# Four accumulation banks with written-out roles, and the second LayerNorm given out in single pieces

## The chip, the cores and the metric

One core of a Trainium2 chip runs the whole kernel. The metric is the device time of one execution in microseconds (us), as the median of several runs. TensorE (PE) does the matrix products, VectorE (DVE) the elementwise work and the statistics of the norms, ScalarE (ACT) copies, roundings and tanh, GpSimd (POOL) the reciprocal square roots, and SyncE (SP) issues nearly all DMAs. Each engine works through its own queue in the order in which the program was written. Engines wait for one another by semaphores.

## The reference

One layer of a streaming encoder on 2048 prompt rows and 32 sample rows of 1024 features. This case lives in the last third of it, the SwiGLU block and the norm behind it:

```python
m, states = mixer(h, ...)                               # recurrent, retention and attention heads
h = layer_norm(ALPHA * h + m, p['ln1_g'], p['ln1_b'])
f = swiglu(h, p['w_gate'], p['w_up'], p['w_down'])      # 1024 -> 2816 -> 1024
h = layer_norm(ALPHA * h + f, p['ln2_g'], p['ln2_b'])

def swiglu(h, w_gate, w_up, w_down):
    a = jnp.einsum('btd,df->btf', h, w_gate)
    b = jnp.einsum('btd,df->btf', h, w_up)
    return jnp.einsum('btf,fd->btd', jax.nn.silu(a) * b, w_down)
```

Everything is float32. The kernel keeps that precision by splitting each operand in a rounded high part and a low rest, and adding three products (high x high, low x high, high x low).

## The kernel before

The span has two halves. Until about 1092 us `run()` works through the mixer, and through SwiGLU for the first 288 rows (block 0). The rest is done in two *parts* s = 0 and 1 of 896 rows each (`PART`, block number `NBLK + s`, that is 6 and 7). Per part there are 22 feature tiles f of 128 columns (`FT`). I write (s, f) for one of them.

**The seven products.** `gu(s, f)` computes gate and up projection of one feature tile by a seven-product scheme (Strassen-Winograd): seven products, each of 12 matmuls of 128x448, that are added into four PSUM banks called by the roles x, z, y, v. In the order of the program they are p1 into x, p5 into z, p6 into y, p2 onto x, p4 into v, p7 onto y, p3 onto z. `multiply` issues the 12 matmuls; the elementwise work on the sums (`after_p1` ... `after_p3`, L1575 to L1607, and `low`, L1611) is written one product later, by `behind` and `catch_up`. So `after_p3` of one tile stands in the queues behind p1 of the next. `gbank` takes each bank from a pool of four buffers, one after another; which buffer a new tile gets is left to the pool.

**The weights.** `background(3)` after each product lets ACT round up to some weight tiles (L1390), DVE subtract to get the rest (L1395) and form sums of weights (L1403), and SP load raw weights (L1372, tile `ww`), store the sums (L1414, part 0) or load stored ones back (L1420, part 1).

**Down products.** After p6 of the tile at which a group of feature tiles ends (f = 3 for the first group of three), `down(s, g)` multiplies the group with the down weights: 2 halves x 7 row tiles, each 9 matmuls of 128x512 into one of four `mm` banks, and `d_add` (L1641 for the first group, L1643 later) adds the bank to the row tile `tok`. A row tile is 128 rows x 1024, 512 KB.

**The second norm as side work.** `ln2(b)` is a generator that normalises the finished rows of block b in place and stores them: L492 statistics of two halves, L493, L494, a power on POOL, then L500 and L502, two passes over the whole row tile. L505 stores it, and only when the store has landed does `load_rows` (L168) load the next part's rows into the freed tile. `y0` = `ln2(0)` has three tiles and runs in (0, 1) to (0, 3); `y6` = `ln2(6)` has seven and runs in (1, 0) to (1, 3). Of the next part's seven row tiles two are loaded at the start of `y6`, and five wait for a store. The last part's norm is written out in `finale`.

**What sets the order.** The order in each queue is fixed when the program is built. `step()` is called after each product and each row tile of `down`. It adds `pace["rate"]` (us of DVE work) to a credit that is kept up to 1.0, and calls `next` on the side generators while the credit is positive; the number that a generator yields is taken off. `pipeline(gens, 2)` starts the next row tile at every second call, and a call advances *all* active row tiles by one stage each. In `down`, a loop advances the norm until the row tile needed is loaded; in the second half it runs the norm to its end.

Where lines of the changed kernel are shown, they stand higher by 2 to 12: 492 became 494 and 496, 493 became 497, 494 498, 500 504, 502 506, 505 509, 1372 1383, 1395 1406, 1403 1414, 1420 1431, 1567 1578, 1589 1600, 1595 1606, 1602 1613, 1603 1614 and 1641 1653.

Of the kernel before, what the change touches and what calls it, by code (L numbers as in the profile page):

```python
# [9 lines left out]
F32 = mybir.dt.float32  # L10
# [21 lines left out]
NBLK = len(BLOCKS)  # L32
# [65 lines left out]
def tile_hybrid_step(ctx: ExitStack, tc: tile.TileContext, io, outs):  # L98
# [33 lines left out]


    tok, arrived = {}, {}
    side, express, pace = {}, {}, {"rate": 1.5, "credit": 0.0, "turn": [], "twice": False, "factor": 1.0, "turns": 0}

    def row_tile():
        return tk.tile([128, D], F32, name="tok", bufs=11)
# [150 lines left out]
    def step():  # L289

        for name, n in list(express.items()):
            for _ in range(n):
                if name in side:
                    advance(name)
        pace["turns"] += 1
        pace["credit"] = min(pace["credit"], 1.0) + pace["rate"]
        for name in pace["turn"][:]:
            if pace["credit"] <= 0.0:
                break
            pace["turn"].remove(name)  # L300
            pace["turn"].append(name)
            pace["credit"] -= advance(name)
# [4 lines left out]
        while pace["turns"] < until:  # L307
            yield 0.0

    def pipeline(gens, every):  # L310

        gens, active, n = list(gens), [], 0
        while gens or active:
            if gens and n % every == 0:
                active.append(gens.pop(0))
            cost = 0.0
            for g in active[:]:
                try:
                    c = next(g)
                    cost += 0.5 if c is None else c  # L320
                except StopIteration:
                    active.remove(g)
            n += 1
            yield cost
# [149 lines left out]
    def ln2(b):  # L474

        after = max(b, NBLK - 1) + 1
        ahead = 11 - 2 - len(ttiles(b))
        mine = tok[b]
        gt, bt = bcast("ln2_g"), bcast("ln2_b")
        here = pace["turns"] + 5  # L480
        n = len(ttiles(b))
        st = sb.tile([128, n, 2, 6], F32, name="ln_st", bufs=2)
        mv = sb.tile([128, n, 2], F32, name="ln_mv", bufs=2)
        rs = sb.tile([128, n], F32, name="ln_rs", bufs=2)
        more = list(range(len(ttiles(after)))) if after < NBLK + NPART else []
        for _ in range(min(ahead, len(more))):
            load_rows(after, (more.pop(0),))

        def tile_(t, c0, rows):
            x = mine[t][:rows, :]  # L490
            for i in range(2):
                dve.bn_stats(st[:rows, t, i, :], x[:, i * 512:(i + 1) * 512])  # L492
            dve.bn_aggr(mv[:rows, t, :], st[:rows, t])  # L493
            dve.tensor_scalar(rs[:rows, t:t + 1], mv[:rows, t, 1:2], EPS, None, op0=ALU.add)  # L494
            yield 1.75
            pool.tensor_tensor(rs[:rows, t:t + 1], rs[:rows, t:t + 1], mhalf[:rows, 0:1], op=ALU.pow)  # L496
            yield 0.1
            while pace["turns"] < here:
                yield 0.0
            dve.scalar_tensor_tensor(x, x, mv[:rows, t, 0:1], gt[:rows, :], op0=ALU.subtract, op1=ALU.mult)  # L500
            yield 1.35
            dve.scalar_tensor_tensor(x, x, rs[:rows, t:t + 1], bt[:rows, :], op0=ALU.mult, op1=ALU.add)  # L502
            yield 1.35
            if c0 < ptok(b):
                sp.dma_start(outs["y"][START[b] + c0:START[b] + c0 + 128, :], x)  # L505
            else:
                sp.dma_start(outs["ys"], x)
            mine[t] = None
            if more:
                load_rows(after, (more.pop(0),))  # L510
            yield 0.0

        yield from pipeline([tile_(t, c0, rows) for t, (c0, rows) in enumerate(ttiles(b))], 2)
        del gt, bt
        while more:
            load_rows(after, (more.pop(0),))
        del tok[b]
# [725 lines left out]
        loads()  # L1243
        start("w0", (need([(0, 0, n)]) and None for n in ("b11", "t1", "t2")))

    def gbank(n=HALF):
        return pg.tile([128, 512], F32, name="gu", bufs=4)[:, :n]

    def two():
        return xp.tile([128, 2, HALF], F32, name="two", bufs=4)  # L1250
# [294 lines left out]
    def behind(*fns):  # L1545

        lag.append(fns)
# [8 lines left out]
    def gu(s, f):  # L1556

        bank, v = {}, {}

        def multiply(n, left, right, first):  # L1560
            if first:
                bank[n] = gbank()
            (wl, wh), = need([(s, f, right)])
            xl, xh = X[left]
            for x, (w, a) in enumerate(((wh, xh), (wl, xh), (wh, xl))):
                for k in range(4):
                    pe.matmul(bank[n], w[:, k * 128:k * 128 + 128], a[:, k, :],  # L1567
                              start=first and x == 0 and k == 0,
                              stop=x == 2 and k == 3, skip_group_check=not first)
            drop([(s, f, right)])  # L1570

        def after_p1():
            x = two()
            v["t1"], v["g1"] = x[:, 0, :], x[:, 1, :]
            act.activation(v["t1"], bank["x"], AF.Copy)  # L1575

        def after_p5():
            x = v["raw"] = two()
            v["u2"], v["p5"] = x[:, 0, :], x[:, 1, :]
            act.activation(v["p5"], bank["z"], AF.Copy)  # L1580

        def after_p6():
            dve.tensor_tensor(v["u2"], v["t1"], bank["y"], op=ALU.add)

        def after_p2():
            act.activation(v["g1"], bank["x"], AF.Tanh, scale=0.5)

        def after_p4():
            dve.scalar_tensor_tensor(v["g1"], v["g1"], 1.0, bank["x"], op0=ALU.add, op1=ALU.mult)

        def after_p7():
            x = two()
            v["c"], v["g2"] = x[:, 0, :], x[:, 1, :]
            v["u3"] = v["t1"]
            dve.tensor_tensor(v["u3"], v["t1"], bank["y"], op=ALU.add)  # L1595
            dve.tensor_tensor(v["c"], v["u3"], bank["v"], op=ALU.subtract)
            dve.tensor_tensor(v["p5"], v["u3"], v["p5"], op=ALU.add)
            act.activation(v["g2"], v["c"], AF.Tanh, scale=0.5)

        def after_p3():  # L1600
            t = GT[f] = xp.tile([128, 2, PART], F32R, name="g", bufs=3)
            dve.tensor_tensor(v["u2"], v["u2"], bank["z"], op=ALU.add)
            dve.scalar_tensor_tensor(v["u2"], v["g1"], 0.5, v["u2"], op0=ALU.mult, op1=ALU.mult)
            dve.scalar_tensor_tensor(v["g2"], v["g2"], 1.0, v["c"], op0=ALU.add, op1=ALU.mult)
            act.activation(t[:, 1, :HALF], v["u2"], AF.Copy)
            dve.scalar_tensor_tensor(v["p5"], v["g2"], 0.5, v["p5"], op0=ALU.mult, op1=ALU.mult)
            act.activation(t[:, 1, HALF:], v["p5"], AF.Copy)  # L1607

        def low():
            t = GT[f]  # L1610
            dve.tensor_tensor(t[:, 0, :], v["raw"].rearrange("p a b -> p (a b)"), t[:, 1, :].bitcast(F32),  # L1611
                              op=ALU.subtract)

        for n, left, right, first, then in (
                ("x", "a11", "b11", True, after_p1), ("z", "s1", "t1", True, after_p5),
                ("y", "s2", "t2", True, after_p6), ("x", "a12", "b21", False, after_p2),
                ("v", "a22", "t4", True, after_p4), ("y", "s3", "t3", False, after_p7),
                ("z", "s4", "b22", False, after_p3)):
            multiply(n, left, right, first)
            catch_up()  # L1620
            behind(then)
            background(3)
            pace["rate"] = 1.3 if s else 0.6
            step()
            if left == "s2":
                for g in due(s, f):
                    down(s, g)
        behind(low)

    def d_part(s, half, t, fs, bank, first, last):  # L1630
# [14 lines left out]
    def down(s, g, more=None):  # L1645
# [3 lines left out]
        for half in range(2):  # L1649
            need([(s, f, half) for f in fs])  # L1650
            banks_ = {}
            if half == 0 and g in ending(s):
                for t in range(5):
                    banks_[t] = mmbank() if t < 4 else gbank(512)
                    d_part(s, half, t, fs[:-1], banks_[t], True, False)
            for t in range(PART // 128):
                if t in banks_:
# [2 lines left out]
                    banks_[t] = mmbank()  # L1660
                    d_part(s, half, t, fs, banks_[t], True, True)
                name = "y0" if s == 0 else f"y{NBLK + s - 1}"
                while name in side and (half or len(tok.get(NBLK + s, ())) <= t):
                    pace["turns"] += 1
                    advance(name)
                catch_up()
# [8 lines left out]
    def finale(s, g):  # L1675
# [55 lines left out]
        every = slice(0, 512)  # L1731
        early = {}
        for t, half in ((0, 0), (0, 1), (1, 0), (1, 1), (2, 0)):
            early[t, half] = mmbank() if len(early) < 4 else gbank(512)
            products(t, half, every, early[t, half], fs[:-1])

        def rest(t, half):
# [41 lines left out]
    run()  # L1779
    rights.close()  # L1780
    sb = rights.enter_context(tc.tile_pool(name="sb2", bufs=1, side="right"))
    pace.update(rate=1.9, credit=0.0, twice=False)
    start("x1", columns_rest(), 2)
    for s_ in range(NPART):
        for f_ in range(FT):
# [119 lines left out]
```

## Time and profile before

| | |
|---|---|
| runs | 2335.75, 2337.96, 2338.66 us; median 2337.96 |
| the profiled execution | 2332.88 us, its span 2330.8 us |
| mean granted TensorE clock | 0.983 |
| PE busy | 2247.1 us, 96% |
| DVE busy | 1480.5 us, 64% |
| ACT busy | 790.7 us, 34% |
| DMA | 417.90 MB, mean 179 GB/s |

The profiled execution is about 5 us faster than the median of the timed runs; sums below are made in the profiled one. A timeline row gives start, duration, engine, line, operation, tiles and, in brackets, the idle time of the engine just before and what ended it. A row with x8 or x2 is a run of equal instructions.

### The profile page before, as it was taken

How to read it: one execution, taken by the hardware profiler on the slowest of the kernel's cores; microseconds unless marked ns; L12 is line 12 of the kernel's file. 1: busy time of each engine (PE TensorE's matmuls, PEld its weight loads, DVE VectorE, ACT ScalarE, POOL GpSimd, SP SyncE). 2: the span in 40 equal slices, each digit the busy share in tenths (PEclk: the TensorE clock that was granted, in tenths of full speed). 3: DMA queues.
4: the chain of work that ended last, by engine and by line, in shares of the span. 5: the costliest groups of instructions: out<-in, count | busy, mean ns of one | idle time of the engine just before them, and what ended most of it. 6: DMA issues, size and time to landing. Idle time of an engine off the chain costs nothing. (4 is left out here: it accounts for less than half of the span.)

```text
span 2330.8 us, 31924 instructions
## 1 busy us (share of the span) xinstructions
PE 2247.1 (96%) x12168; PEld 1959.1 (84%) x12168; DVE 1480.5 (64%) x2656; ACT 790.7 (34%) x1585; POOL 154.9 (7%) x236
## 2 busy tenths in 40 slices
PE   8999999999999999989899999999989999999995
PEld 7887878988888889868788898888877888898884
DVE  7795757566446376567865776677785544454557
ACT  5645263351523334234332332233421221221221
POOL 2010201101001011000000000000000000000003
PEclk9999999999999999999999999999999999999998
DMA  6563676767759665764643443344555443343341
GB/s 220 177 201 104 232 261 209 279 221 247 264 181 323 245 215 173 252 207 159 229 161 114 149 158 127 118 145 138 196 172 193 132 149 105 121 149 118 126 136 63
DMA packets 139272, 417.90 MB, mean 179 GB/s; under 512 B 20272, under 2 KB 35440, under 8 KB 127472
## 3 DMA queue, kind: packets, MB, share of 16 engines
q1 hardware_dynamic: 119056, 407.35, 51.1%
q10 hardware_dynamic: 20064, 8.52, 1.3%
q8 instruction: 96, 1.57, 0.3%
q14 instruction: 56, 0.46, 0.1%
HBM read 316.55 MB, written 99.26 MB: 178 GB/s over the span
## 5 line engine op out<-in xcount | busy, mean ns | idle before, releaser
L1567 PE MATMUL gu<-xh,pair 128*128 128x448 f32 x2464 | 559.6, 369 | 19.1 <-DVE two L1595 7.8
L1567 PEld LDWEIGHTS gu<-xh,pair 128*128 128x128 f32 x2464 | 466.2, 190 | 64.2 <-issue 8.8
L904 PE MATMUL mm<-hAh,pair 128*128 128x384 f32 (+2 forms) x2432 | 425.0, 323 | 16.4 <-DVE pair L254 5.8
L904 PEld LDWEIGHTS mm<-hAh,pair 128*128 128x128 f32 x2432 | 376.7, 192 | 41.3 <-issue 17.9
L1390 ACT ACTIVATE pair<-ww 128x512 fp32r<-128x512 f32 x308 | 189.7, 626 | 519.0 <-PE mm L1636 230.7
L1395 DVE TENSOR_TENSOR pair<-ww,pair 128x512 fp32r<-128x512 f32 x308 | 208.4, 689 | 155.3 <-ACT pair L1390 154.4
L1567 PE MATMUL gu<-xl,pair 128*128 128x448 f32 x1232 | 303.8, 368 | 0.1
L1567 PEld LDWEIGHTS gu<-xl,pair 128*128 128x128 f32 x1232 | 233.0, 189 | 21.4 <-DVE xl L1319 1.0
L1643 DVE TENSOR_TENSOR tok<-tok,mm 128x512 f32<-128x512 f32 x181 | 124.2, 688 | 161.1 <-PE mm L1636 160.0
L1634 PE MATMUL mm<-pair,g 128*128 128x512 f32 x571 | 225.1, 394 | 0.2 <-DVE tok L1641 0.2
L1635 PE MATMUL mm<-pair,g 128*128 128x512 f32 x571 | 225.2, 394 | 0.0
L1636 PE MATMUL mm<-pair,g 128*128 128x512 f32 x571 | 224.5, 393 | 0.0
L904 PE MATMUL mm<-hAl,pair 128*128 128x384 f32 (+2 forms) x1216 | 211.9, 317 | 0.0
L250 ACT ACTIVATE pair<-stage 128x1024 fp32r<-128x1024 f32 x131 | 138.1, 1055 | 189.2 <-DMA stage<-in_wgu 57.2
L904 PEld LDWEIGHTS mm<-hAl,pair 128*128 128x128 f32 x1216 | 193.2, 193 | 0.3 <-DVE hAl L1129 0.2
L254 DVE TENSOR_TENSOR pair<-stage,pair 128x1024 fp32r<-128x1024 f32 x130 | 158.2, 1218 | 32.8 <-ACT pair L250 32.6
L1634 PEld LDWEIGHTS mm<-pair,g 128*128 128x128 f32 x571 | 107.3, 188 | 25.5 <-DVE tok L1641 0.7
L1636 PEld LDWEIGHTS mm<-pair,g 128*128 128x128 f32 x571 | 107.4, 188 | 25.0
L1635 PEld LDWEIGHTS mm<-pair,g 128*128 128x128 f32 x571 | 107.3, 188 | 24.2
L991 PE MATMUL mm<-pair,hCh 128*128 128x512 f32 x216 | 90.3, 418 | 6.1 <-DVE tok L1022 3.5
L993 PE MATMUL mm<-pair,hCh 128*128 128x512 f32 x216 | 86.4, 400 | 1.3 <-DVE pair L254 1.3
L992 PE MATMUL mm<-pair,hCl 128*128 128x512 f32 x216 | 86.3, 399 | 0.5 <-DVE hCl L974 0.5
(296 smaller groups left out, 2633.2 us busy)
## 6 DMA issues: line engine op xcount, KB each, us to landing
pair<-keptW SPq DMA_DIRECT2D x63, 1024.0 KB, 5.4
ww<-in_wgu SPq DMA_DIRECT2D x154, 256.0 KB, 3.2
pair<-keptO SPq DMA_DIRECT2D x28, 1024.0 KB, 4.8
stage<-in_win SPq DMA_DIRECT2D x45, 512.0 KB, 4.6
stage<-in_wgu SPq DMA_DIRECT2D x44, 512.0 KB, 4.2
ww<-in_wdn SPq DMA_DIRECT2D x88, 256.0 KB, 3.1
keptW<-pair SPq DMA_DIRECT2D x36, 512.0 KB, 8.0
stage<-in_wdn SPq DMA_DIRECT2D x22, 512.0 KB, 3.8
```

What stands on the lines that cost most here:

```text
L250: act.activation(whi[u], staged[u], AF.Copy)
L254: eng.tensor_tensor(wlo[u], staged[u], whi[u].bitcast(F32), op=ALU.subtract)
L904: pe.matmul(p, w[:, k, :], a[:, k, :], start=(x == 0 and k == 0), stop=(x == 2 and k == 7))
L991: pe.matmul(o, ah[:, cs], wh[:, x, :], start=first and x == 0, stop=False)
L993: pe.matmul(o, ah[:, cs], wl[:, x, :], start=False, stop=last and x == 1)
L1390: act.activation(pairs[key][1], whole_w[x], AF.Copy)
L1395: dve.tensor_tensor(pairs[key][0], whole_w[x], pairs[key][1].bitcast(F32), op=ALU.subtract)
L1567: pe.matmul(bank[n], w[:, k * 128:k * 128 + 128], a[:, k, :], start=first and x == 0 and k == 0, stop=x == 2 and k == 3, skip_group_check= ...
L1634: pe.matmul(bank, gh, wh, start=first and f == fs[0], stop=False)
L1635: pe.matmul(bank, gl, wh, start=False, stop=False)
L1636: pe.matmul(bank, gh, wl, start=False, stop=last and f == fs[-1])
L1643: dve.tensor_tensor(r, r, bank, op=ALU.add)
```

## The change

Three things:

1. `gbank` names four tiles `gu0` to `gu3` of one buffer each, and `turn_banks` swaps the roles after each feature tile: x keeps its bank, z takes y's, y takes v's, v takes z's.
2. `pipeline(..., apart=True)` in `ln2`: a call returns after *one* row tile's stage of 0.5 us or more instead of after a stage of every active tile. The statistics become two stages (0.7 and 1.05). From the seven products on no credit is kept (`most` 0.0 for 1.0), and the rate in part 1 is 1.5 for 1.3.
3. In `down` the norm is no longer run to its end in the second half; only the row tile that is needed is waited for, in both halves.

```diff
-        pace["credit"] = min(pace["credit"], 1.0) + pace["rate"]
+        pace["credit"] = min(pace["credit"], pace["most"]) + pace["rate"]
...
-    def pipeline(gens, every):
+    def pipeline(gens, every, apart=False):
...
                     cost += 0.5 if c is None else c
+                    if apart and cost >= 0.5:
+                        yield cost
+                        cost = 0.0
...
-            for i in range(2):
-                dve.bn_stats(st[:rows, t, i, :], x[:, i * 512:(i + 1) * 512])
+            dve.bn_stats(st[:rows, t, 0, :], x[:, 0:512])
+            yield 0.7
+            dve.bn_stats(st[:rows, t, 1, :], x[:, 512:1024])
...
-            yield 1.75
+            yield 1.05
...
-        yield from pipeline([...], 2)
+        yield from pipeline([...], 2, True)
...
-    def gbank(n=HALF):
-        return pg.tile([128, 512], F32, name="gu", bufs=4)[:, :n]
+    gbanks = {"x": 0, "z": 1, "y": 2, "v": 3}
+
+    def gbank(role, n=HALF):
+        return pg.tile([128, 512], F32, name="gu%d" % gbanks[role])[:, :n]
+
+    def turn_banks():
+
+        x, z, y, v = (gbanks[r] for r in "xzyv")
+        gbanks.update(x=x, z=y, y=v, v=z)
...
-            pace["rate"] = 1.3 if s else 0.6
+            pace["rate"] = 1.5 if s else 0.6
...
+        turn_banks()
...
-                while name in side and (half or len(tok.get(NBLK + s, ())) <= t):
+                while name in side and len(tok.get(NBLK + s, ())) <= t:
...
-    pace.update(rate=1.9, credit=0.0, twice=False)
+    pace.update(rate=1.9, credit=0.0, twice=False, most=0.0)
```

The queues of PE, ACT and POOL hold the same instructions in the same order as before. On DVE and SP they differ in two places, around `y0` and around `y6`.

**First place: DVE in (1, 1), just behind p1.** L1595 to L1597 are `after_p7` of (1, 0), L1602 and L1603 the start of its `after_p3`. Before:

```order
L1595 TENSOR_TENSOR two<-two,gu 128x448
L1596 TENSOR_TENSOR two<-two,gu 128x448
L1597 TENSOR_TENSOR two<-two 128x448
L1395 TENSOR_TENSOR pair<-ww,pair 128x512
L502 SCALAR_TENSOR_TENSOR tok<-tok,ln_rs 128x1024 x2
L500 SCALAR_TENSOR_TENSOR tok<-tok,ln_mv 128x1024
L492 BN_STATS ln_st<-tok 128x6 x2
L493 BN_AGGR ln_mv<-ln_st 128x2
L494 TENSOR_SCALAR ln_rs<-ln_mv 128x1
L1602 TENSOR_TENSOR two<-two,gu 128x448
```

and in the changed kernel:

```order
L1606 TENSOR_TENSOR two<-two,gu_15382 128x448
L1607 TENSOR_TENSOR two<-two,gu_15424 128x448
L1608 TENSOR_TENSOR two<-two 128x448
L1406 TENSOR_TENSOR pair<-ww,pair 128x512
L504 SCALAR_TENSOR_TENSOR tok<-tok,ln_mv 128x1024
L1613 TENSOR_TENSOR two<-two,gu_15363 128x448
```

Norm work of four row tiles stood ahead of `after_p3`; now one pass over one row tile does.

**Second place: DVE in (0, 2), around p1.** L1589 is `after_p4` of (0, 1), L1595 the first of its `after_p7`. Before:

```order
L1395 TENSOR_TENSOR pair<-ww,pair 128x512
L1589 SCALAR_TENSOR_TENSOR two<-two,gu 128x448
L1403 TENSOR_TENSOR ww<-ww 128x512
L1395 TENSOR_TENSOR pair<-ww,pair 128x512
L500 SCALAR_TENSOR_TENSOR tok<-tok,ln_mv 128x1024 x2
L492 BN_STATS ln_st<-tok 32x6 x2
L493 BN_AGGR ln_mv<-ln_st 32x2
L494 TENSOR_SCALAR ln_rs<-ln_mv 32x1
L1595 TENSOR_TENSOR two<-two,gu 128x448
```

and in the changed kernel:

```order
L1406 TENSOR_TENSOR pair<-ww,pair 128x512
L494 BN_STATS ln_st<-tok 128x6
L1600 SCALAR_TENSOR_TENSOR two<-two,gu_10897 128x448
L1414 TENSOR_TENSOR ww<-ww 128x512
L1406 TENSOR_TENSOR pair<-ww,pair 128x512
L1606 TENSOR_TENSOR two<-two,gu_10953 128x448
```

The norm's work ahead of `after_p7` is gone, and one statistic now stands ahead of `after_p4`.

**Third place: SP around (1, 3) and its `down`.** `tok<-rows` is the load of a row tile of part 1, `out_y<-tok` the store of a finished one. Before, from the third store on:

```order
L505 DMA out_y<-tok 128x1024
L168 DMA tok<-rows_8424 128x1024
L1372 DMA ww<-in_wdn 128x512 x2
L1420 DMA pair<-sum3t_11013 128x1024
L505 DMA out_y<-tok 128x1024
L168 DMA tok<-rows_9620 128x1024
L1420 DMA pair<-sum3t_11035 128x1024
L1372 DMA ww<-in_wdn 128x512 x2
L505 DMA out_y<-tok 128x1024
L168 DMA tok<-rows_9622 128x1024
L1372 DMA ww<-in_wgu 128x512 x3
```

and in the changed kernel, from the raw weights ahead of the third store:

```order
L1383 DMA ww<-in_wgu 128x512 x5
L509 DMA out_y<-tok 128x1024
L168 DMA tok<-rows_8424 128x1024
L509 DMA out_y<-tok 128x1024
L168 DMA tok<-rows_9620 128x1024
L509 DMA out_y<-tok 128x1024
L168 DMA tok<-rows_9622 128x1024
L1431 DMA pair<-sum3t_11238 128x1024
L1431 DMA pair<-sum3t_11256 128x1024
```

The last three exchanges of a finished row tile for a new one stood among the weight loads of (1, 2) and (1, 3); now they stand together behind those loads, and the last two weight pairs of (1, 3) behind them.

More of the change, by code (lines that the diff above doesn't have):

```diff
@@ L134, in tile_hybrid_step @@
     tok, arrived = {}, {}
-    side, express, pace = {}, {}, {"rate": 1.5, "credit": 0.0, "turn": [], "twice": False, "factor": 1.0, "turns": 0}
+    side, express, pace = {}, {}, {"rate": 1.5, "credit": 0.0, "turn": [], "twice": False, "factor": 1.0, "turns": 0, "most": 1.0}
     def row_tile():
@@ L511, in tile_ @@
             yield 0.0
-        yield from pipeline([tile_(t, c0, rows) for t, (c0, rows) in enumerate(ttiles(b))], 2)
+        yield from pipeline([tile_(t, c0, rows) for t, (c0, rows) in enumerate(ttiles(b))], 2, True)
         del gt, bt
@@ L1561, in multiply @@
             if first:
-                bank[n] = gbank()
+                bank[n] = gbank(n)
             (wl, wh), = need([(s, f, right)])
@@ L1653, in down @@
                 for t in range(5):
-                    banks_[t] = mmbank() if t < 4 else gbank(512)
+                    banks_[t] = mmbank() if t < 4 else gbank("x", 512)
                     d_part(s, half, t, fs[:-1], banks_[t], True, False)
@@ L1733, in finale @@
         for t, half in ((0, 0), (0, 1), (1, 0), (1, 1), (2, 0)):
-            early[t, half] = mmbank() if len(early) < 4 else gbank(512)
+            early[t, half] = mmbank() if len(early) < 4 else gbank("x", 512)
             products(t, half, every, early[t, half], fs[:-1])
```

## Prediction

> **What bounds the kernel now.** I read the windows of the seven products' half first, then PE's waits in the two windows in which PE is not full, then the timelines there. Columns of a window: length, busy time of PE, PEld, DVE, ACT, POOL with counts, granted clock, DMA share, GB/s.
>
> ```profile
> 1115.00:1145.00 30.00, 23.25 (x104) 20.17 (x103) 24.54 (x42) 9.90 (x19) 1.81 (x3) 0.94 0.68 257
> 1145.00:1695.00 550.00, 549.78 (x2569) 481.86 (x2567) 382.88 (x583) 172.91 (x306) 0.00 (x0) 1.00 0.43 147
> ...
> 1704.00:1775.00 71.00, 60.63 (x269) 53.69 (x268) 55.32 (x87) 17.95 (x35) 4.23 (x7) 0.90 0.63 210
> 1775.00:2290.00 515.00, 515.00 (x2411) 452.51 (x2410) 255.41 (x398) 113.61 (x206) 0.99 (x2) 1.00 0.39 127
> ```
>
> For 550 and 515 us PE is full and the clock is 1.00; nothing that moves DVE or SP work there can pay. The holes are at (0, 1) to (0, 2) and at (1, 0) to (1, 3), where `y0` and `y6` run, and POOL's few powers show it. How large are they? The same view for the products' matmuls alone (PE, PEld, clock, DMA share, GB/s):
>
> ```profile
> 1715.48:1722.83 7.35, 7.35 (x37) 6.57 (x35) 1.00 0.42 161
> 1705.10:1772.33 67.23, 56.95 (x253) 50.70 (x251) 0.90 0.63 209
> 1114.27:1145.51 31.24, 24.50 (x110) 21.32 (x109) 0.95 0.69 256
> ```
>
> The first row is three undisturbed products, 36 matmuls (one more reaches in): 2.45 us for a product. The second runs from p2 of (1, 0) to the first down product, 21 products: 67.23 - 21 x 2.45 = 15.8 us lost. The third runs from p6 of (0, 1) to p4 of (0, 2), 9 products: 31.24 - 22.05 = 9.2 us lost. These 25 us are all that the change can win. PE's waits in 1704 to 1775:
>
> ```profile
> PE gu L1567 <- ACT two L1575: 5.0, 1, 5.0
> PE gu L1567 <- DVE two L1595: 3.9, 1, 3.9
> PE gu L1567 <- DMA pair<-sum2t: 1.0, 1, 1.0
> ```
>
> **The waits of part 1, and why they go.** The longest one, in four timelines (DVE, ACT, PE):
>
> ```profile
> 1713.19 2.48 DVE L500 SCALAR_TENSOR_TENSOR tok<-tok,ln_mv 128x1024 f32<-128x1024 f32 x2
> 1715.59 0.61 DVE L1595 TENSOR_TENSOR two<-two,gu 128x448 f32<-128x448 f32 x1
> ...
> 1718.69 2.47 DVE L502 SCALAR_TENSOR_TENSOR tok<-tok,ln_rs 128x1024 f32<-128x1024 f32 x2
> ...
> 1723.91 0.61 DVE L1602 TENSOR_TENSOR two<-two,gu 128x448 f32<-128x448 f32 x1
> ```
> ```profile
> 1725.21 0.58 ACT L1605 ACTIVATE g<-two 128x448 fp32r<-128x448 f32 x1 [7.16 <-DVE two L1603]
> ...
> 1727.41 0.53 ACT L1575 ACTIVATE two<-gu 128x448 f32<-128x448 f32 x1
> ```
> ```profile
> 1727.98 3.36 PE L1567 MATMUL gu<-xh,pair 128*128 128x448 f32 x8 [4.97 <-ACT two L1575]
> ...
> 1732.63 1.84 PE L1567 MATMUL gu<-xh,pair 128*128 128x448 f32 x8
> ```
>
> PE names ACT, but ACT sat idle 7.16 us for DVE, and DVE spent 1718.69 to 1723.91 on the norm: 5.2 us for four row tiles in one step. Behind that stand L1602, then ACT's L1605 and L1607, then L1575, which p2 needs before it adds onto x. After the wait 12 matmuls take 1727.98 to 1732.63, 4.65 us for 2.45: a wait costs its length and then 2.2 us of half clock. In the changed order one L500 stands there, (1715.59 - 1713.19) / 2 = 1.2 us, so L1602 comes 4.0 earlier, and 2.4 more because the two L500 ahead of L1595 are gone. L1575 would start at about 1721; PE reaches p2 at 1722.83. The wait goes, with some 1.5 us to spare. The wait for `pair<-sum2t` and the 3.9 for L1595 have another root, on SP:
>
> ```profile
> SPq L168 <- DMA out_y<-tok: 28.8, 5, 6.7
> ```
> ```profile
> 1741.07 0.32 SPq L168 DMA_DIRECT2D tok<-rows  x1
> 1741.44 0.42 SPq L505 DMA_DIRECT2D out_y<-tok  x1
> 1747.47 0.32 SPq L168 DMA_DIRECT2D tok<-rows  x1
> ...
> 1756.30 0.42 SPq L505 DMA_DIRECT2D out_y<-tok  x1
> 1763.48 0.32 SPq L168 DMA_DIRECT2D tok<-rows  x1
> ...
> 1765.34 0.42 SPq L505 DMA_DIRECT2D out_y<-tok  x1
> 1771.90 0.33 SPq L168 DMA_DIRECT2D tok<-rows  x1
> 1772.66 1.28 SPq L1372 DMA_DIRECT2D ww<-in_wgu  x3
> ...
> 1774.51 1.56 SPq L1372 DMA_DIRECT2D ww<-in_wgu  x2
> ```
>
> A load waits in SP's queue until the store of the same row tile has landed, 6.03, 7.18 and 6.56 us in these rows, and the weight loads behind it wait along: 28.8 us in five exchanges. In the changed order two exchanges stand among the weights of (1, 1) to (1, 3), about 14 us apart, and three stand behind them. I take all 15.8 us as gone from this stretch; the cover for the two exchanges left is that weights are asked for a tile ahead.
>
> **What is late next.** `down` of (1, 3) then starts at 1772.33 - 15.8 = 1756.5, but the new rows come later. One row tile of it takes 2.09 us, from 14 tiles in this window:
>
> ```profile
> 1772.33:1801.58 29.25, 29.25 (x128) 23.82 (x127) 14.49 (x20) 1.90 (x3) 0.00 (x0) 1.00 0.44 144
> ```
>
> The five raw loads were done 3.7 us after `down` began (1774.51 + 1.56 - 1772.33), so the third store is issued at about 1760.3. A store behind raw loads takes 6.9 (mean of 7.18 and 6.56), one behind a row load 6.03, and the next store follows a load by 0.4. So the loads are issued at 1767.2, 1767.6 + 6.0 = 1773.6 and 1774.0 + 6.0 = 1780.0. A row load lands after 3.6:
>
> ```profile
> tok<-rows SPq DMA_DIRECT2D x5, 512.0 KB, 3.6
> ```
>
> That is 1777.2 and 1783.6 for the last two, and with one add of 0.7 and 0.1 of signalling the `mm` banks of the sixth and seventh tile are free at 1778.0 and 1784.4. There are four banks, so the tenth tile waits for the sixth: nominal 1756.5 + 9 x 2.09 = 1775.3, wait 2.7. The eleventh waits for the seventh: 1780.1, wait 4.3. With one half-clock stretch of 2.2 that is 9.2 us. Part 1 gains 15.8 - 9.2 = **6.6**. The ends: no new wait at all (15.8), or the longest exchange shown, 7.18 three times: 2.6 us less, 4.0. The weight pairs behind the exchanges are issued at 1781 and needed at p4, 1756.5 + 29.25 + 9.2 + 2.45 = 1797: covered.
>
> **Part 0.** Timeline rows of DVE and PE:
>
> ```profile
> 1126.81 0.69 DVE L1403 TENSOR_TENSOR ww<-ww 128x512 f32<-128x512 f32 x1 [2.98 <-DMA ww<-in_wgu]
> ...
> 1128.02 0.61 DVE L1589 SCALAR_TENSOR_TENSOR two<-two,gu 128x448 f32<-128x448 f32 x1
> ...
> 1130.59 2.48 DVE L500 SCALAR_TENSOR_TENSOR tok<-tok,ln_mv 128x1024 f32<-128x1024 f32 x2
> ...
> 1134.59 0.60 DVE L1595 TENSOR_TENSOR two<-two,gu 128x448 f32<-128x448 f32 x1
> ...
> 1138.34 0.61 DVE L1602 TENSOR_TENSOR two<-two,gu 128x448 f32<-128x448 f32 x1
> ```
> ```profile
> 1128.78 1.85 PE L1567 MATMUL gu<-xh,pair 128*128 128x448 f32 x8 [1.03 <-DVE two L1589]
> ...
> 1135.33 3.27 PE L1567 MATMUL gu<-xh,pair 128*128 128x448 f32 x8 [3.89 <-DVE two L1595]
> ...
> 1142.94 1.91 PE L1567 MATMUL gu<-xh,pair 128*128 128x448 f32 x8 [0.95 <-ACT two L1575]
> ```
>
> The clock of this place is the landing at 1126.8, which no norm moves: what is won ahead of it is waited for here. Behind it a statistic (0.6) now stands ahead of L1589, so p1 of (0, 2) starts at 1129.4. L1595 takes the place of the L500: 1131.2, and p5 starts without a wait when p1 ends, 1131.9. p2 then waits for L1575 behind `after_p3`: L1602 comes at 1131.2 + 3.75 + 1.2 for one L500 = 1136.1, 2.2 us earlier, so p2 starts at 1140.7 for 1142.94, after a wait of 4.0. The gain is 2.2 if no half clock follows, and 0 if one does. The 3.89 us wait here was followed by a slow p5, but that was hidden ahead of the wait at p2. Up to 0.9 more can go to passes among the first adds of `down` (of 1.2 each beside tiles of 2.09). I take **1.0**, from -1.0 to 2.2. In the Trainium skill, TensorE: Matmul & The Clock Gate, Part 1: The HAM clock gate, the array falls to half clock after an idle window of about 3.4 us. By that rule the 4.0 us wait at p2 would cost the half clock, and the sum would be 6.6 instead of 7.6; the 4.97 us wait above agrees.
>
> **What costs nothing.** DVE runs the same work in smaller pieces, with no instruction more, and PE, ACT and POOL keep their order. The rate of 1.5 and the credit only place the pieces. The written-out banks I price at 0: p5 of (0, 2) was released at 1135.33 by L1595, the last reader of y, three us ahead of L1602, the last reader of z. So z already took y's bank: the pool did the swap.
>
> **Sum.** 6.6 + 1.0 = 7.6 us. The profiled execution took 2332.88 us and would take 2325.3; the median of the runs is 5.1 higher, and from it I get 2337.96 - 7.6 = **2330.4**.
>
> **The rivals.** (a) *The stores are quick in a quiet queue.* For it speaks that stores of the same size take half as long elsewhere:
>
> ```profile
> sum3t<-pair SPq DMA_DIRECT2D x4, 512.0 KB, 3.5
> ```
>
> With 3.5 the last load is bound by DVE's passes; it lands at about 1777.6, the eleventh tile waits 1.1, and the gain is 15.8 - 1.1 + 1.0 = 15.7: 2322.3. Against it: each of the three stores has a 512 KB load or raw loads just ahead of it. In the Trainium skill, DMA: Bandwidth & Descriptors, Anatomy of one DMA, a DMA costs 2.0 us and its bytes by 436 GB/s; 3.2 us here by that rule, an estimate from that page which goes with this rival, and which the 6 us stores of these rows do not bear out.
>
> (b) *The exchanges eat the gain.* Other row stores took 8.0:
>
> ```profile
> rows<-tok SPq DMA_DIRECT2D x16, 512.0 KB, 8.0
> ```
>
> Three at 8.0 are 5.0 more than 19.0, the gain is 2.6, and it ends at 2335.4, no change that can be measured (0.2%, 4.7 us, is about what a measurement here can tell).
>
> (c) *Slower.* The same place, with one price: from 7.6 us more in the chain of three stores and a load the eleventh tile waits longer than all that was won. At 9.6 a store and 6.0 for the load (9.8 + 2.4 more) it is 2342.6. No row shows such a store; against it is that SP issues nothing else meanwhile.
>
> (d) *The banks matter,* and p5 is freed one product earlier all along. The row at 1135.33 excludes it, and in 550 us of full PE there is no wait to win.
>
> **How the numbers follow.** The forecast's case has 0.57, (a) 0.12, (b) 0.21, (c) 0.09, (d) 0.01. The forecast's own range is the ends 4.0 and 9.5 of part 1 (one short wait without half clock) with part 0: 2326.5 to 2334.5. For 8 in 10 I reach into (a) and (b): 2323.5 to 2337.0. Faster by over 0.2%: the forecast's case but for its slow end (0.03), and (a): 0.66; same 0.25; slower 0.09.
>
> **What would show it.** No wait of PE over 1 us between 1704 and the first down product; instead two waits of `mm` L1634 for L1641's adds, about 2.7 and 4.3 us, and five waits of SP for `out_y`. In part 0 one wait of about 2.7 at p1 and one of 2 to 4 at p2 of (0, 2). The prediction is wrong if a wait stays at the products of (1, 1) to (1, 3), or if the exchange takes under 5 or over 8 us.

## The result, and the profile after

| | before | changed |
|---|---|---|
| runs, median (lowest to highest) | 2337.72 us (2335.75 to 2338.66, 4 runs) | 2319.66 us (2317.79 to 2322.29, 4 runs) |
| ratio | | 0.9937, 95% interval 0.9918 to 0.9957 |
| the profiled execution, its span | 2332.88, 2330.8 us | 2317.79, 2315.8 us |
| mean granted TensorE clock | 0.983 | 0.984 |

The change is worth 18.1 us in the medians and 15.0 in the two profiled spans. Forecast were 7.6 us, 2330.4. On a second chip the same pair stood at 2332.46 and 2319.58 us (e8), 12.9 apart. The direction was right; the gain is about twice the forecast, and the time lies below the range.

The windows of the products' matmuls in the changed kernel, for the two places of the prediction (length, busy time of PE and PEld, granted clock, DMA share, GB/s):

```profile
1703.94:1755.14 51.20, 51.20 (x253) 47.12 (x251) 1.00 0.68 234
1115.28:1144.60 29.32, 24.21 (x109) 21.36 (x108) 0.94 0.73 273
```

The 21 products from p2 of (1, 0) to the first down product take 51.20 us for 67.23: nothing is lost any more. In part 0 the nine products take 29.32 for 31.24. PE's waits of the changed kernel in 1704 to 1790, and then in 1115 to 1145:

```profile
PE mm L1646 <- DVE tok L1653: 1.8, 1, 1.8
```
```profile
PE gu L1578 <- DVE two L1600: 2.9, 1, 2.9
PE gu L1578 <- ACT two L1586: 2.2, 1, 2.2
```

The three waits of part 1 are gone, and one new one is there, in `down`. The place at which 5.0 us were lost, in timeline rows of DVE, ACT and PE:

```profile
1715.16 1.28 DVE L504 SCALAR_TENSOR_TENSOR tok<-tok,ln_mv 128x1024 f32<-128x1024 f32 x1
1716.36 0.62 DVE L1613 TENSOR_TENSOR two<-two,gu 128x448 f32<-128x448 f32 x1
```
```profile
1719.87 0.53 ACT L1586 ACTIVATE two<-gu 128x448 f32<-128x448 f32 x1
```
```profile
1721.01 1.80 PE L1578 MATMUL gu<-xh,pair 128*128 128x448 f32 x8
```

One pass of the norm stands ahead of `after_p3` (L1613). `after_p1` (L1586) ends at 1720.40, and p2 begins at 1721.01 without a wait, 0.6 us later. What is late next, `down` of (1, 3), as a window of all engines and as SP's timeline, with SP's wait for the stores:

```profile
1755.14:1786.33 31.19, 29.37 (x127) 23.59 (x126) 26.46 (x40) 2.61 (x5) 2.62 (x3) 1.00 0.54 186
```
```profile
1747.78 11.36 SPq L1383 DMA_DIRECT2D ww<-in_wgu  x5
1759.18 0.43 SPq L509 DMA_DIRECT2D out_y<-tok  x1
1763.64 0.33 SPq L168 DMA_DIRECT2D tok<-rows  x1
1764.56 0.34 SPq L509 DMA_DIRECT2D out_y<-tok  x1
1768.56 0.32 SPq L168 DMA_DIRECT2D tok<-rows  x1
1770.38 0.34 SPq L509 DMA_DIRECT2D out_y<-tok  x1
1773.57 0.32 SPq L168 DMA_DIRECT2D tok<-rows  x1
```
```profile
SPq L168 <- DMA out_y<-tok: 20.3, 5, 6.1
```

From store to load it is 4.46, 4.00 and 3.19 us, where the kernel before had 6.03 to 7.18. The first store, at 1728.88, goes out behind two weight loads of 512 KB issued in the 2.8 us ahead of it and takes 6.58. The five waits sum to 20.3 us for 28.8. So the last load goes out at 1773.57, and only the eleventh tile waits, behind the add of the seventh (DVE, PE):

```profile
1777.21 1.29 DVE L1653 SCALAR_TENSOR_TENSOR tok<-tok,mm 128x512 f32<-128x512 f32 x2 [3.26 <-DMA tok<-rows]
```
```profile
1777.95 0.49 PE L1646 MATMUL mm<-pair,g 128*128 128x512 f32 x1 [1.82 <-DVE tok L1653]
```

`down` takes 31.19 us for the undisturbed 29.25: 1.9 lost, where 9.2 were forecast.

### The profile page after: what moved, and what is told of

The parts are those of the page before. It is cut to its first block, busy times and chain, and to the rows that moved or that the text cites. A ratio compares the mean times of both kernels' runs of the same rounds, so it can differ in the third digit from the quotient of the medians.

```text
span 2315.8 us, 31921 instructions
## 1 busy us (share of the span) xinstructions
PE 2243.0 (97%) x12168; PEld 1956.8 (84%) x12168; DVE 1479.7 (64%) x2656; ACT 790.6 (34%) x1585; POOL 158.0 (7%) x236
## 4 chain that ended last, share of the span: by engine, by line
PE 25%; issue 22%; DVE 3%; DMA 1%; POOL 0%; ACT 0%; SPq 0%; DVEq 0%; ACTq 0%; POOLq 0%
PE gu L1578 16%; PE mm L1647 3%; PE mm L1646 3%; PE mm L1648 3%; DVE end_st L1713 0%; DVE tok L1711 0%; DVE end_mv L1721 0%; POOL end_rs L1718 0%; DMA pair<-sum3t 0%; DVE pair L1406 0%; DMA out_y<-tok 0%; DVE xl L1330 0%; DVE tok L1733 0%; DMA tok<-rows 0%; DVE tok L1333 0%
```

## Experiments

"The 21 products" below are always those from p2 of (1, 0) to the first down product: 67.23 us before, 51.20 in the changed kernel.

### e1 to e4: which part of the change carries it

e1 is the kernel before with the pieces alone:

```diff
+                    if apart and cost >= 0.5:
+                        yield cost
+                        cost = 0.0
...
+            yield 0.7
...
-        yield from pipeline([...], 2)
+        yield from pipeline([...], 2, True)
```

> The kernel before with one thing of the change: the norm's generator returns after one row tile's stage, and the statistics are two stages. Credit up to 1.0, rate 1.3 and the run to the end in `down` stay as before. Theory A (what PE waited for was the burst of norm work of several row tiles in one step): almost the whole effect of the change, 12 to 16 us faster in the span, no wait of PE over 1 us between 1705 us and the first down product, `down` of (1, 3) 30 to 32 us long. Theory B (the credit carries it: a call may still be followed by a second one in the same place): at most a third of the effect, 2 to 6 us, and waits of PE for DVE of 2 us and more stay among the products of (1, 1) to (1, 3).

Measured: 2319.23 us, ratio 0.9951 (0.9935 to 0.9967), beside 2332.25 before on that chip. The 21 products take 51.42 us, and PE's waits from 1704 to 1792 are

```profile
PE mm L1638 <- DVE tok L1645: 3.1, 1, 3.1
PE gu L1571 <- DVE xl L1323: 0.3, 1, 0.3
```

The pieces alone bring the whole effect. `down` takes 32.6 us, just above the 30 to 32 that theory A gave it.

e2 is the kernel before with the credit alone:

```diff
-        pace["credit"] = min(pace["credit"], 1.0) + pace["rate"]
+        pace["credit"] = min(pace["credit"], pace["most"]) + pace["rate"]
...
+    pace.update(rate=1.9, credit=0.0, twice=False, most=0.0)
```

> The kernel before with one thing of the change: no credit is kept from the seven products on. A call still advances all active row tiles by a stage. Theory A (the size of one call's burst decides): only a part of the effect, 3 to 9 us faster, since a call of 3 to 5 us of DVE work still stands between the adds; several PE waits of 1 to 3 us for DVE remain in (1, 1) to (1, 3). Theory B (credit decides): 12 us or more faster, no such wait.

Measured: 2322.98 us, ratio 0.9964 (0.9950 to 0.9978), 9.3 us under before. Half clock means below that the granted clock falls to a half and matmuls take about twice as long. The window of the 21 products, and DVE's largest burst in it:

```profile
1703.29:1759.50 56.21, 52.75 (x253) 46.64 (x251) 1.00 0.68 227
```
```profile
1721.61 2.48 DVE L502 SCALAR_TENSOR_TENSOR tok<-tok,ln_rs 128x1024 f32<-128x1024 f32 x2
...
1726.83 0.62 DVE L1583 TENSOR_TENSOR two<-two,gu 128x448 f32<-128x448 f32 x1
```

This is just above the 9 us of theory A, and it shows more than either theory said: of the several waits of 1 to 3 us that theory A expected only one is over 1 us, 1.3 for L1583. The burst is as large as before, 5.2 us (1721.61 to 1726.83, for 1718.69 to 1723.91 before). But it stands ahead of L1583 (`after_p6`) instead of L1602 (`after_p3`). Of 15.8 us lost, 4.8 are left (56.21 - 51.45), and the clock stays at 1.00. So the credit moved the largest burst and did not make it smaller. How much of the 11 us comes from this and how much from the changed order on SP, e2 does not separate; e9 and e10 test the place of a burst directly.

e3 is the kernel before with the banks alone:

```diff
-                bank[n] = gbank()
+                bank[n] = gbank(n)
...
+        turn_banks()
```

> The kernel before with the written-out banks alone. Theory A (the pool's own rotation gives z the bank of y, y that of v and v that of z already): no difference, within 0.2%, and the same waits of PE as before (5.0, 3.9 and 1.0 us in 1704 to 1775). Theory B (the roles free p5 a product earlier): some us faster, and the waits for L1595 go.

Measured: 2332.66 us, ratio 1.0003 (0.9990 to 1.0017). PE's waits have the same two large entries as before:

```profile
PE gu L1574 <- ACT two L1582: 5.0, 1, 5.0
PE gu L1574 <- DVE two L1602: 4.3, 1, 4.3
```

The banks do nothing.

e4 is the changed kernel with the run to the end in `down` put back:

```diff
-                while name in side and len(tok.get(NBLK + s, ())) <= t:
+                while name in side and (half or len(tok.get(NBLK + s, ())) <= t):
```

> The changed kernel with the run of the norm to its end in the second half of `down` put back. Theory A (the norm is through its row tiles by then, so nothing is left to run): the time of the changed kernel, 2315 to 2323 us, and `down` of (1, 3) again 31 us long. Theory B (the run to the end is a burst of its own): 2 to 5 us slower than the changed kernel, with a wait of PE for DVE in the second half of `down`.

Measured: 2319.77 us, ratio 0.9954 (0.9936 to 0.9972); the 21 products 51.18 us, `down` 33.0 us with one wait of 2.0 for L1653 and a half clock. Theory A holds in the time; its 31 us for `down` was missed by that half clock. The rate of 1.5 was not run alone; e1, which leaves it at 1.3, has the whole effect without it.

### e5 and e6: the size of a store

Both are the changed kernel with one (e5) or two (e6) more stores of the same row tile to a scratch place ahead of each of the last three stores of `y6`:

```diff
+                for i in range(1 if b == NBLK and t in (2, 3, 4) else 0):   # e6: 2
+                    sp.dma_start(dr.tile([128, D], F32, name=f"again{t}{i}"), x)
                 sp.dma_start(outs["y"][START[b] + c0:START[b] + c0 + 128, :], x)
```

> The changed kernel, but each of the last three row tiles of part 0 that are exchanged in `y6` is first stored once more to a scratch place in DRAM, 512 KB right ahead of its own store in SP's queue. Theory A (a store takes as long as what stands ahead of it in the queues: 6 to 7 us behind weight loads in the kernel before, 3.2 to 4.5 us in the changed kernel, whose queue is quiet there): at 418 GB/s, the busiest stretch in the trace, 512 KB are 1.25 us, so store to load becomes 4.4 to 5.8 us for these three, the last load comes about 3.8 us later, and `down` of (1, 3) takes 34 to 36 us instead of 31.2. Theory B (the time of a store is latency and not shared bandwidth): store to load stays 3.2 to 4.5, `down` 31 to 32.

> As the run before, with two extra stores of 512 KB ahead of each of the three. Theory A: store to load 5.7 to 7.0 us, which is what the kernel before showed and the prediction had put in; the last load about 7.5 us later than in the changed kernel; `down` of (1, 3) 38 to 41 us, with a wait of PE for the adds of L1653's line over 4 us, and a half clock behind it. Theory B: as the changed kernel, 31 to 32 us.

SP's last exchange and PE's wait in `down`, first of e5 and then of e6:

```profile
1770.27 0.32 SPq L510 DMA_DIRECT2D again<-tok  x1
1770.64 0.42 SPq L511 DMA_DIRECT2D out_y<-tok  x1
1776.63 0.32 SPq L168 DMA_DIRECT2D tok<-rows  x1
```
```profile
PE mm L1648 <- DVE tok L1655: 4.8, 2, 2.6
```
```profile
1779.17 0.91 SPq L510 DMA_DIRECT2D again<-tok  x2
1780.12 1.25 SPq L511 DMA_DIRECT2D out_y<-tok  x1
1786.90 0.32 SPq L168 DMA_DIRECT2D tok<-rows  x1
```
```profile
PE mm L1648 <- DVE tok L1655: 8.6, 2, 5.1
```

Store to load is 5.12, 5.83 and 5.99 us in e5 and 5.72, 6.65 and 6.78 in e6, for 4.46, 4.00 and 3.19. `down` takes 37.58 and 41.22 us at a clock of 0.91 and 0.92 (one execution each: 2322.27 and 2332.25 us). Theory A holds against theory B, but two of e5's three exchanges are above its 5.8, e5's `down` is above its 34 to 36, since each of the two waits was followed by half clock, and e6's `down` is just above 41. In e5 the last load goes out 23.2 us after `down` began, where the forecast had 23.5, and the forecast's own picture appears: waits at the tenth and the eleventh tile, slow matmuls behind, and 37.58 us for `down` where the forecast's is 29.25 + 9.2 = 38.45. The mechanism was right, the size of the store was not.

### e7, e8 and e11: the wait of part 0

e7 lets `ln2` issue one row load in each round of its stages instead of all at its start; e11 does so for `y0` alone. e8 is the changed kernel again, beside e7.

```diff
-        for _ in range(min(ahead, len(more))):
-            load_rows(after, (more.pop(0),))
+        first = [more.pop(0) for _ in range(min(ahead, len(more)))]
+        def rows_in():
+            for t in first:
+                load_rows(after, (t,))
+                yield 0.0
...
-        yield from pipeline([tile_(...) ...], 2, True)
+        yield from pipeline([rows_in()] + [tile_(...) ...], 2, True)
```

> The changed kernel, but `ln2` no longer issues all its first row loads at once (six for `y0`, two for `y6`): one goes out in each round of the norm's stages. Theory A (the wait of DVE for `ww` until 1128 us in the changed kernel, and with it both waits of PE in (0, 2), 3.1 and 2.3 us, come from 4 MB of norm vectors and rows that stand in SP's queue ahead of that weight load): both waits go, p6 of (0, 1) to p4 of (0, 2) takes 23 to 26 us instead of 29.3, and the kernel is 3 to 6 us faster than the changed one. Theory B (the norm's pieces on DVE set it, or the spread loads meet other weight loads later): the waits stay or move to (0, 2) and (0, 3); within 2 us of the changed kernel.

> The changed kernel itself, once more beside the others on this chip. Both theories: 2316 to 2323 us.

> As the run with spread row loads, but for `y0` alone; `y6` loads its two tiles at once as in the changed kernel. Theory A (the spread is worth what the one wait in (0, 2) costs, and the longer `down` of (1, 3) in that run, 33.3 us, came from the spread in `y6`): p6 of (0, 1) to p4 of (0, 2) 25 to 27 us, `down` of (1, 3) 30.5 to 31.5, the time 3 to 5 us under the changed kernel. Theory B (the difference in `down` is the scatter of store times): `down` anywhere from 30.5 to 33.5, the time 1 to 4 us under the changed kernel.

Measured: e7 2317.15 us, ratio 0.9937 (0.9917 to 0.9957); e8 2319.58, ratio 0.9945 (0.9933 to 0.9957), both beside 2332.46 before; e11 2316.83, ratio 0.9916 (0.9896 to 0.9935), beside 2334.49. In the changed kernel DVE waits for a raw weight tile, behind the six row loads in SP's queue (rows of SP and DVE):

```profile
1114.13 3.41 SPq L168 DMA_DIRECT2D tok<-rows  x6
```
```profile
1128.09 0.69 DVE L1414 TENSOR_TENSOR ww<-ww 128x512 f32<-128x512 f32 x1 [4.39 <-DMA ww<-in_wgu]
```

The window of the nine products of part 0 in e11, all engines:

```profile
1115.92:1141.80 25.88, 23.64 (x109) 21.40 (x108) 22.38 (x36) 10.62 (x21) 0.55 (x1) 0.94 0.88 307
```

The first of the two waits goes (25.9 us in e7 and e11, for 29.3 in the changed kernel and 30.8 in e8); one of 2.2 at p2 stays, so theory A of e7 holds for one of its two waits. So the late weight load was held up by the six row loads that the norm's generator issues in one go. `down` of (1, 3) took 33.3, 30.5 and 32.9 us in e7, e8 and e11: there theory A of e11 missed, and the scatter of theory B fits. e7 is 2.4 us under the changed kernel beside it, less than the 3 to 6 expected; e11 has the lowest ratio of all, but its interval still touches those of the changed kernel, so a gain in the whole time is not shown.

### e9 and e10: the same burst in two places

The changed kernel with extra stages of `y6` in one step:

```diff
             step()
+            if (s, f, left) == (1, 0, "s4"):     # e9;  e10: (1, 1, "s2") and range(4)
+                for _ in range(6):
+                    advance("y6")
```

> The changed kernel with one burst put back: in the step after p3 of (1, 0) six more stages of `y6` are given out, so that 5.3 us of norm work (three L504 or L506 passes of 1.2, statistics of 1.7) stand on DVE ahead of `after_p3`, instead of one pass of 1.2. Theory A (the place decides: `after_p3` and ACT's `after_p1` behind it have 1.5 us to spare ahead of p2): a PE wait of 2 to 4 us at p2 of (1, 1), 1 to 2.2 us of half clock behind it, the 21 products from p2 of (1, 0) to the first down product take 54 to 57 us instead of 51.2. Theory B (what counts is the norm work in the whole stretch, not its pieces): no wait over 1 us, 51 to 52 us.

> The changed kernel with a burst of the same size (5.2 us: two passes, three statistics) in another place: in the step after p6 of (1, 1), ahead of `after_p6` on DVE. Theory A (the place decides: the bank that `after_p6` reads is written again only by p7, two products or 4.9 us later): a wait of at most 1.5 us, 51 to 53 us for the 21 products. Theory C (a burst of 5 us costs its excess wherever it stands): a wait of 2 to 4 us here too, 54 to 57 us.

The window of the 21 products, PE's wait, and the first row of DVE's burst with the add behind it, of e9 and then of e10:

```profile
1699.74:1755.65 55.91, 52.59 (x245) 47.98 (x243) 0.94 0.66 227
```
```profile
PE gu L1578 <- ACT two L1586: 3.3, 1, 3.3
```
```profile
1709.31 1.28 DVE L504 SCALAR_TENSOR_TENSOR tok<-tok,ln_mv 128x1024 f32<-128x1024 f32 x1
...
1714.55 0.61 DVE L1613 TENSOR_TENSOR two<-two,gu 128x448 f32<-128x448 f32 x1
```
```profile
1706.98:1759.22 52.24, 51.46 (x253) 47.04 (x251) 1.00 0.70 248
```
```profile
PE gu L1578 <- DVE two L1594: 0.8, 1, 0.8
```
```profile
1724.11 0.69 DVE L496 BATCH_NORM_STATS2 ln_st<-tok 128x6 f32<-128x512 f32 x1
...
1729.21 0.62 DVE L1594 TENSOR_TENSOR two<-two,gu 128x448 f32<-128x448 f32 x1
```

5.2 us of norm work ahead of `after_p3`, for 1.2 in the changed kernel, cost 4.7 us (55.91 - 51.20), 3.3 of wait and the rest half clock; 5.1 us ahead of `after_p6`, for 2.3, cost 1.0. Theory A holds in both: the place decides. Both kernels then have no wait in `down`, since their last row load goes out 13.5 and 15.2 us after `down` began instead of 18.4. The whole time does not show the difference: e9's one execution took 2316.03 us, e10's 2319.68, and e9 had come to part 1 5.8 us earlier than the changed kernel's profiled execution.

### e12 and e13: the exchanges out of SP's queue

e12 is the kernel before, e13 the changed one, with the stores of `y6` and the loads that wait for them issued by POOL:

```diff
-                sp.dma_start(outs["y"][START[b] + c0:START[b] + c0 + 128, :], x)
+                (pool if b == NBLK else sp).dma_start(outs["y"][START[b] + c0:START[b] + c0 + 128, :], x)
...
-                load_rows(after, (more.pop(0),))
+                load_rows(after, (more.pop(0),), pool if b == NBLK else None)
```

> The kernel before with one thing changed: in part 1 the stores of `y6` and the row loads that wait for them are issued by POOL's queue instead of SP's. The norm's bursts stay. Theory A (the 3.9 us wait for L1595 in (1, 3) and the 1.0 us wait for `pair<-sum2t` come from weight loads that stand behind a waiting row load in SP's queue): these two waits go or fall under 1.5 us, the 5.0 us wait at p2 of (1, 1) stays, the 21 products take 58 to 62 us instead of 67.2, the time falls by 4 to 8 us. Theory B (they come from DVE's bursts as the first one does): all three waits stay, 66 to 68 us. A miss that is possible: powers on POOL now stand behind the waiting row loads, and DVE waits for them.

> The changed kernel with the stores of `y6` and the row loads that wait for them issued by POOL's queue; DVE's order stays. Theory A (in the changed kernel the three last exchanges stand alone, each set by the DVE pass ahead of it and by the store's 3 to 4.5 us): `down` of (1, 3) is 30 to 32.5 us as with SP's queue, the time that of the changed kernel within 0.2%. Theory B (SP's order still holds the exchanges or the weights back): `down` under 30 us, 1 to 3 us faster. Against both: weight loads that SP no longer holds back run beside the stores and make them longer, 5 to 7 us, `down` 33 us and more.

e12: 2327.72 us, ratio 0.9965 (0.9952 to 0.9978), 6.8 us under before; the 21 products take 59.74 us, and of PE's waits the burst's own is left:

```profile
PE gu L1567 <- ACT two L1575: 4.9, 1, 4.9
PE gu L1567 <- DVE two L1583: 0.4, 1, 0.4
```

So of the 15.8 us some 7.5 (67.23 - 59.74) had their root in SP's queue and some 8.3 in the burst, as the prediction had read it.

e13: 2323.39 us, ratio 0.9953 (0.9937 to 0.9968); the 21 products are clean (51.2), but `down` takes 36.79. SP's timeline, POOL's, and PE's wait:

```profile
1765.67 1.03 SPq L1431 DMA_DIRECT2D pair<-sum3t  x2
```
```profile
1761.92 0.58 POOL L509 DMA_DIRECT2D out_y<-tok  x1 [1.50 <-DVE tok L506]
1765.26 0.54 POOL L168 DMA_DIRECT2D tok<-rows  x1 [2.76 <-DMA out_y<-tok]
...
1767.24 0.58 POOL L509 DMA_DIRECT2D out_y<-tok  x1
1774.64 0.53 POOL L168 DMA_DIRECT2D tok<-rows  x1 [6.81 <-DMA out_y<-tok]
```
```profile
PE mm L1646 <- DVE tok L1653: 6.0, 1, 6.0
```

The third outcome that was named came. SP, no longer held, issues two weight loads of 512 KB 1.6 us ahead of the last store; that store takes 7.40 us from store to load, and PE waits 6.0. POOL's queue as such is not what makes it slow: the store before it, in the same queue, takes 3.34 us (1761.92 to 1765.26). In the changed kernel the same two loads stand behind the last exchange. The waiting row load in SP's queue, which cost the kernel before its weights, keeps the stores of the changed kernel quick. In the Trainium skill, DMA: Bandwidth & Descriptors, Issuing engines are not separate DMA queues, DMAs of several issuing engines run on the same 16 DMA engines and interleave; the 7.40 us beside 3.34 agree.

e14 joins e13's edit with e11's.

> Spread row loads of `y0` and the exchanges of `y6` on POOL's queue together. Theory A: the gain of the spread alone, 2 to 4 us under the changed kernel, 2314 to 2318 us. Theory B: 1 to 3 us more, 2312 to 2315 us.

Measured: 2318.74 us, ratio 0.9932 (0.9919 to 0.9944): above the ranges of both theories, and nothing over the spread alone. `down` takes 37.4 us here too.

## Why the prediction was wrong, point by point

**Where the loss was: right.** 15.8 us in part 1 and its two roots (e9, e12); all of it went, as forecast. ACT's L1586 ended 0.6 us ahead of p2, less than half of the 1.5 us to spare that was forecast.

**What is late next: the right place, the wrong size.** The step that failed is the price of the three exchanges: a store behind raw loads at 6.9 us, one behind a row load at 6.03, and the next store 0.4 behind a load. Measured: 4.46, 4.00 and 3.19, and 0.9 and 1.8 between a load and the next store. With these sizes the wait in `down` was 1.9 us and not 9.2. The third store went out 4.0 us after `down` began (forecast 3.8), a row load landed after 3.6, and the eleventh tile waited, as worked out; the tenth did not. What the rows that gave 6.9 had ahead of them shows in SP's timeline of before, just ahead of the store at 1756.30:

```profile
1754.50 0.32 SPq L168 DMA_DIRECT2D tok<-rows  x1
1754.91 0.86 SPq L1372 DMA_DIRECT2D ww<-in_wdn  x2
1755.86 0.38 SPq L1420 DMA_DIRECT2D pair<-sum3t  x1
```

A row load and 1 MB of weights (two of 256 KB, one of 512 KB) within 1.8 us. In the changed order the raw loads ahead of the third store go out one by one, as DVE frees their tiles, over 11.36 us; in the 2 us ahead of that store there are two of 256 KB, at 1757.62 and 1758.81. For the two stores behind it SP is held at the waiting load, so that no weight load can stand there, and each goes out later behind the row load, since it waits for DVE's second pass (L506). That SP issues nothing else meanwhile stands in the prediction, but only as an argument against the slower rival; it should have sized the store. So rival (a) was the case, by its own mechanism. The fifth store took 3.19 with a row load 1.8 us ahead of it; with nothing issued in the 4.9 us ahead, the last store of e10 that a load waits for took 2.63 (1771.80 to 1774.43). e5, e6 and e13 show the way from there up to 7.40. In the Trainium skill, DMA: Bandwidth & Descriptors, Anatomy of one DMA, the rule of 2.0 us and the bytes by 436 GB/s, from which the prediction worked out 3.2, is given for DMAs issued by GpSimd; SP's stores took 3.19 and 2.63 here, at it and below.

**The sum of the miss.** Forecast and measured median are 10.7 us apart. 7.3 of it are this term (9.2 - 1.9). Part 0 gave 1.9 for 1.0, and `down` of (0, 3) 0.5 more. 3.2 come from the base: the profiled run of before lay 5.1 below its median, that of the changed kernel 1.9 below its own. Against it, the products of part 0 began 1.0 later. That makes 10.9, within 0.2 of the miss.

**Part 0: right.** Waits of about 2.7 and 2 to 4 were forecast; 2.9 and 2.2 came, with the half clock hidden ahead of the second. In e8 it was 3.0 and 3.6, and the nine products took 30.79 us, so the gain of 1.9 is not sure. But the landing at 1126.8 that "no norm moves" is set by the norm's own row loads (e7, e11).

**What costs nothing.** The banks: right (e3). The rate: not run alone, but nothing is missing without it (e1). The credit, said to "only place the pieces", was put at nothing, but it alone is worth 11 of the 16 us of part 1 (e2). It did not spoil the sum only because the pieces alone also do all of it (e1); that is luck.

**The range** ended at 2323.5, with 0.12 for rival (a). The row nearest in kind (a store of the same line) was taken over the row nearest in its surroundings (a 512 KB store in a quiet queue, 3.5). The 9.5 at the range's fast end of part 1 does not come out of the prediction's terms: the wait of 4.3 alone would leave 11.5.

## What to carry to other kernels

Price a moved DMA by what will stand beside it in the new order, above all by what its own queue can and cannot issue meanwhile, and not by the same line's duration in the old order. For side work among the products, ask which add stands behind it and when PE needs that add: 5 us ahead of one cost 4.7 us, ahead of another 1.0. A wait in a shared queue may be what keeps traffic off the next transfer, so look at what it holds back before it is taken out.

## What the runs showed of the hardware

Whether a wait of PE is followed by half clock is no matter of its length alone. At the switch of columns ahead of part 1, all sixteen profiled executions have the same wait of 2.0 us; behind eleven of them the matmuls run at half clock, behind five (e1, e2, e4, e9, e13) they don't. The changed kernel and e1:

```profile
1697.27 2.26 PE L1578 MATMUL gu<-xh,pair 128*128 128x448 f32 x6 [2.03 <-ACT xh L1327]
```
```profile
1698.19 1.50 PE L1571 MATMUL gu<-xh,pair 128*128 128x448 f32 x6 [2.03 <-ACT xh L1320]
```

Six matmuls take 2.26 us in the one and 1.50 in the other. At this place the half clock cost nothing: p2 of (1, 0) starts 6.67 us behind the wait in both, since in e1 PE waits another 1.24 and 0.28 us for the low parts of the columns. Between 1092 and 1172 us and between 1690 and 1802 us, all seventeen waits of 3.2 us and more in the sixteen executions were followed by half clock; of the shorter ones some were (2.67 us in e4) and some were not (3.17 us in e10).

In the Trainium skill, TensorE: Matmul & The Clock Gate, Part 1: The HAM clock gate, half clock follows an idle window of about 3.4 us; here it also followed 2.0 us, so the measurement decides against that length as a lower limit for a wait. The same section of the Trainium skill says that the window runs freely, which would let equal waits fall differently; no run here shows the window.

For an estimate this means that a wait of over 3.2 us carries half clock, and one of 2 to 3.2 us may carry it or not. What it costs depends on the next wait: 2.2 us behind the 4.97 us wait of the prediction, nothing at the switch of columns. How much of the scatter of the times comes from it was not measured; 20 runs of the kernel before on one chip spread from 2325.76 to 2338.89 us.
